# Mixer B's scores: the pass over k's low half as two products of 64 rows, one for each half of the keys

## The chip, the cores and the metric

The kernel runs on one core of one Trainium2 chip. What is measured is the device time of one execution in microseconds; before the change it is 1545.34 us, the median of three runs (1544.65 to 1547.67). On such a core, TensorE (PE) multiplies matrices and transposes, VectorE (DVE), ScalarE (ACT) and GpSimd (POOL) work on tiles, and SyncE (SP) issues DMAs. Each engine runs its own queue of instructions in order and waits for others by semaphores. TensorE reads from SBUF and writes to PSUM, whose banks hold 512 float32 numbers for each of 128 partitions.

## The reference

A trunk of two layers over 1024 tokens of width 1024. Each layer: RMS norm, one projection to q, k, v and a gate, a token mixer, an output projection and a residual, then a gated per-layer embedding. Layer 0 has mixer A (neighbourhood attention), layer 1 has mixer B, which the change touches: 16 query heads of 64 dimensions share 4 heads of k and v, with normalised and rotated q and k.

```python
def q_block(qb):
    sc = jnp.einsum('bkgqd,bksd->bkgqs', qb, k).astype(jnp.float32) * scale
    pr = jax.nn.softmax(sc, axis=-1).astype(v.dtype)
    return jnp.einsum('bkgqs,bksd->bkgqd', pr, v)
```

So for each query head and each block of 128 queries there are 128 x 1024 scores, a softmax over the 1024 keys, and a product with v.

## The kernel before

**Numbers in two parts.** All is float32, but TensorE multiplies in float32r, a rounded float32. Each operand is therefore held as a high part (rounded) and a low part (what the rounding left), and a product is the sum of high by high, high by low and low by high. For most products that is three matmuls (`split3`).

**Mixer B's scores.** A head has only 64 dimensions, and the array has 128 rows, so high and low share them. For each pair of query heads and each half of the queries (`hf`, 512 of them), `q_stack` transposes q, copies it out of PSUM to `raw`, and for each head `j` of the pair fills a tile QS: in the head's own 64 partitions (`own`) ACT writes the high part (line 1068), and two ticks later DVE writes the low part into the other 64 (`oth`, line 1069). On k's side, for each of the 4 KV heads, KA holds k's high part twice, in both halves of the partitions, and KB k's low part twice (`k_stack`; the second copies are POOL's, lines 1005 and 1006). A product of QS with KA over 128 rows then gives (q high + q low) by k high, and one with KB gives (q high + q low) by k low. `f_S` does this for a block of 128 queries: two products of 512 keys each over KA, then two over KB, into a PSUM tile `s` of two banks, one for each 512 keys. All four use the same columns of QS as the stationary operand, and every matmul brings its own weight load.

**The steps.** Mixer B's attention is 128 steps (16 heads, 2 halves of the queries, 4 blocks). At step n PE gets the transposes of P of step n (`f_T`, line 1105), the scores of step n+2 (`f_S`) and at every second step the product with v of the two steps before (`f_AV`, tile `o`). Between them DVE takes the minimum of the scores (they are negated, line 1089), ACT the exponential (line 1095), and both copy the transposed P as high and low part (1107, 1108). `mix` puts dense projections between the attention's items so that both lists end together: the q of the next group, the gates, and the embedding's product. `q_stack` is called 5 steps ahead of the scores that first need it (`QS_AT`); its two high parts are written 4 and 6 ticks later (`QO`), a tick being one item of the attention's list. In the prologue (`pro[0]`) they are written at once.

**POOL's queue in Mixer B** has the rotary products of the next group's q and k (lines 923 to 926), their reciprocal roots and scalings (325, 957), the copies of KA and KB, and for each finished pair of heads the gate and the normalisation of Y (513, 514); the latter waits for a broadcast `rb` that comes through DRAM.

All matmuls except the transposes go through the helper `mm`, so they all have line 317; they are told apart by their tiles: `s` the scores, `d` the projections, `o` mostly the products with v, `t` the transposes.

Of the kernel before, what the change touches and what calls it, by code (L numbers as in the profile page):

```python
# [12 lines left out]
F32R = mybir.dt.float32r  # L13
# [28 lines left out]
QD = (2, 5, 8)  # L42
# [113 lines left out]
def trunk(ctx, tc, x, xT, wts, bias, gains, gain0, hgains, mask, rope, out):  # L156
    nc = tc.nc
    sync, act, dve, pool, pe = nc.sync, nc.scalar, nc.vector, nc.gpsimd, nc.tensor
# [101 lines left out]
    q = WQ.q  # L260
# [55 lines left out]
    def mm(ps, a, b, first, last):  # L316
        pe.matmul(ps, a, b, start=first, stop=last, skip_group_check=True)  # L317
# [560 lines left out]
    def mixer_b(pend):  # L878
        with ExitStack() as es:
# [4 lines left out]
            sb = es.enter_context(tc.tile_pool(name="bsb", bufs=2))  # L884
# [16 lines left out]
            KA, KB, V, QT, QST, P, RS, OP = {}, {}, {}, {}, {}, {}, {}, {}  # L901
# [152 lines left out]
            def q_stack(pair, hf):  # L1054
                g = pair // 2
                ps = psT.tile([128, 4, 128], F32, name="t")
                c = slice((pair % 2) * 128, (pair % 2) * 128 + 128)
                for t in range(4):
                    pe.transpose(ps[:, t], QT[g, hf][:, t, c], ident)  # L1059
                raw = sb.tile([128, 512], F32, name="th")  # L1060
                act.activation(raw, ps.rearrange("p t c -> p (t c)"), AF.Copy)
                for j in range(2):
                    own, oth = slice(64 * j, 64 * j + 64), slice(64 - 64 * j, 128 - 64 * j)
                    qs = sb.tile([128, 512], F32R, name="QS", bufs=3)
                    QST[2 * pair + j, hf] = qs

                    def high(qs=qs, own=own, oth=oth):
                        act.activation(qs[own], raw[own], AF.Copy)
                        post.add(DQ, lambda: dve.tensor_tensor(qs[oth], raw[own], qs[own], ALU.subtract))
                    if pro[0]:  # L1070
                        high()
                    else:
                        post.add(QO[j], high)
# [5 lines left out]
            def f_S(h, hf, t):  # L1079
                g = h // 4  # L1080
                ps = psS.tile([128, 1024], F32, name="s")
                qt = QST[h, hf][:, t * 128:(t + 1) * 128]
                for kk, kt in enumerate((KA[g], KB[g])):
                    for c in range(2):
                        mm(ps[:, c * 512:(c + 1) * 512], qt, kt[:, c * 512:(c + 1) * 512], kk == 0, kk == 1)
                if t == 0:
                    RS[h, hf] = sb.tile([128, 4], F32, name="rs", bufs=3)
                mn = sb.tile([128, 1], F32, name="mn", bufs=3)
                dve.tensor_reduce(mn, ps, axis=AX.X, op=ALU.min)  # L1089
                P[h, hf, t] = (ps, mn)  # L1090
# [38 lines left out]
            pre = kv[:-2] + qi[:6] + kv[-2:-1] + qi[6:10] + kv[-1:] + qi[10:14]  # L1129
            fill = qi[14:] + [d for hf in range(2) for d in gate_items("bg", 0, hf, dalloc, sb, gg)]  # L1130
            pre += [glue(lambda: q_stack(0, 0))] + fill[:5]
            pre += [glue(lambda: f_S(*steps[0]))] + fill[5:6] + [glue(lambda: f_E(*steps[0]))] + fill[6:7]
            pre += [glue(lambda: f_S(*steps[1]))] + fill[7:]
            for i, d in enumerate(pre):
                if i >= 2 and i % 2 == 0 and pend:
# [6 lines left out]
            for g in range(4):  # L1142
                att = []
                for n in range(32 * g, 32 * g + 32):
                    h, hf, t = steps[n]
                    av = n >= 2 and n % 2 == 0
                    w = CB if av else CN
                    att.append((later.tick, w[0]))
                    if av:
                        att.append((lambda n=n: f_AV(*steps[n - 1]), w[1]))  # L1150
                    te = [(lambda n=n: f_T(*steps[n]), w[2])]
                    if n + 1 < len(steps):
                        te.append((lambda n=n: f_E(*steps[n + 1]), w[3]))
                    if n % 2 == 0:
                        te.reverse()
                    att += te
                    if n + 2 < len(steps):
                        att.append((lambda n=n: f_S(*steps[n + 2]), w[4]))
                    m = n + QS_AT
                    if m % 8 == 0 and m < len(steps):  # L1160
                        hn, fn, _ = steps[m]
                        att.append((lambda hn=hn, fn=fn: q_stack(hn // 2, fn), 0.0))
                    if YLOAD_B <= n < YLOAD_B + NT:
                        att.append((lambda t=n - YLOAD_B: load_y(1, t), 0.0))
# [184 lines left out]
```

## Time and profile before

| | before |
|---|---|
| median of 3 runs | 1545.34 us |
| the profiled execution | 1544.88 us |
| its span, from first to last instruction | 1543.1 us |
| mean granted TensorE clock | 0.997 |
| instructions in the trace | 24012 |

The profile is of one execution. Its page gives each engine's busy time, the chain of work that ended last, and groups of instructions by line and tile; the trace behind it can be asked for a stretch of time, for one tile, for waits, or for instructions in order of time. A matmul's duration in the trace runs from its start to a modelled end and overlaps with the next one's; weight loads (PEld) are shown beside the matmuls. The lines that matter are shown in the prediction.

### The profile page before, as it was taken

To read this page: it belongs to the slowest core of one execution; us is meant where nothing else is said; L and a number is where in the kernel's file an instruction comes from. 1 tells how busy PE (TensorE), PEld (TensorE's weight loads), DVE (VectorE), ACT (ScalarE), POOL (GpSimd) and SP (SyncE) were. 2 spreads that over 40 slices of the span, in tenths; PEclk is the share of its full clock that TensorE was granted. 3 is DMA by queue.
4 is the path that set the end of the run, shared out by engine and by line. 5 is a ranking of instruction groups with operands and counts; after the bars stand their busy time and mean duration, and the time that the engine had idled before them with its cause. 6 is when DMAs were issued, how large, how long until landed. Compare 5 with 4: busy or idle time off the path is not lost.

```text
span 1543.1 us, 24012 instructions
## 1 busy us (share of the span) xinstructions
PE 1513.8 (98%) x9016; PEld 1324.3 (86%) x9016; DVE 963.5 (62%) x1638; ACT 847.5 (55%) x1696; POOL 350.6 (23%) x468
## 2 busy tenths in 40 slices
PE   8999999999999999999999999999999999999998
PEld 8789888988988788888988889989899888788886
DVE  4675676566576435556867776677777877624533
ACT  7564555455466423333467676767767767622422
POOL 1231232223122010000432233545041300000124
PEclk9999999999999999999999999999999999999999
DMA  7211312221124961232210111102111213651213
GB/s 300 79 61 47 96 50 67 68 73 60 62 78 124 352 220 44 89 130 79 85 36 22 39 60 41 51 25 69 40 31 42 76 46 118 225 200 55 71 59 130
DMA packets 85635, 138.97 MB, mean 90 GB/s; under 512 B 12816, under 2 KB 49808, under 8 KB 85520
## 3 DMA queue, kind: packets, MB, share of 16 engines
q1 hardware_dynamic: 80912, 122.77, 24.0%
q10 hardware_dynamic: 4608, 14.68, 2.7%
q8 instruction: 71, 1.16, 0.3%
q14 instruction: 44, 0.36, 0.1%
HBM read 104.80 MB, written 32.62 MB: 89 GB/s over the span
## 4 chain that ended last, share of the span: by engine, by line
PE 84%; DVE 6%; ACT 5%; issue 3%; DMA 1%; POOL 1%; ACTq 0%; POOLq 0%; SPq 0%; DVEq 0%
PE d L317 54%; PE o L317 10%; PE s L317 9%; PE t L1105 6%; PE t L686 2%; DVE PTl L1108 1%; PE t L427 1%; DVE mn L1089 1%; ACT PTh L1107 1%; DVE wl L221 1%; ACT P L1095 1%; ACT wh L220 1%; POOL xn L416 1%; PE t L1059 0%; DMA ppD<-G 0%
## 5 line engine op out<-in xcount | busy, mean ns | idle before, releaser
L317 PE MATMUL d<-wh,HTh 128*128 128x256 f32 (+1 forms) x1064 | 358.7, 341 | 5.3 <-ACT wh L232 2.7
L317 PE MATMUL d<-wh,HTl 128*128 128x256 f32 (+1 forms) x1064 | 352.2, 335 | 0.0
L317 PE MATMUL d<-wl,HTh 128*128 128x256 f32 (+1 forms) x1064 | 352.1, 335 | 0.0
L1108 DVE TENSOR_TENSOR PTl<-t,PTh 128x512 fp32r<-128x512 f32 x256 | 164.4, 683 | 124.1 <-ACT PTh L1107 123.6
L317 PEld LDWEIGHTS d<-wh,HTh 128*128 128x128 f32 x1064 | 200.0, 190 | 28.5 <-ACT wh L232 3.0
L317 PEld LDWEIGHTS d<-wl,HTh 128*128 128x128 f32 x1064 | 200.0, 190 | 21.4
L317 PEld LDWEIGHTS d<-wh,HTl 128*128 128x128 f32 x1064 | 199.8, 190 | 21.6
L317 PE MATMUL d<-HTh,wh 128*128 128x512 f32 x504 | 205.7, 408 | 0.0
L317 PE MATMUL d<-HTh,wl 128*128 128x512 f32 x504 | 198.7, 394 | 0.0
L317 PE MATMUL d<-HTl,wh 128*128 128x512 f32 x504 | 197.7, 392 | 0.0
L1095 ACT ACTIVATE P<-s,mn 128x1024 f32<-128x1024 f32 x128 | 142.8, 1115 | 58.2 <-DVE mn L1089 57.5
L1107 ACT ACTIVATE PTh<-t 128x512 fp32r<-128x512 f32 x256 | 139.9, 594 | 43.5 <-PE t L1105 42.5
L1089 DVE TENSOR_REDUCE mn<-s 128x1 f32<-128x1024 f32 x128 | 154.8, 1209 | 11.7 <-PE s L317 11.6
L1105 PE MATMUL t<-ident,P 128*128 128x128 f32 x1024 | 137.4, 275 | 6.7 <-DVE PTl L1108 4.9
L1105 PEld LDWEIGHTS t<-ident,P 128*128 128x128 f32 x1024 | 114.7, 141 | 22.5 <-DVE PTl L1108 16.6
L317 PE MATMUL s<-KA,QS 128*128 128x512 f32 (+2 forms) x384 | 133.7, 402 | 0.0
L221 DVE TENSOR_TENSOR wl<-wstage,wh 128x1024 fp32r<-128x1024 f32 x86 | 107.5, 1255 | 26.7 <-ACT wh L220 25.7
L317 PE MATMUL s<-KB,QS 128*128 128x512 f32 (+2 forms) x384 | 121.6, 371 | 0.0
L317 PE MATMUL o<-PTh,V 128*128 128x256 f32 (+2 forms) x672 | 118.8, 288 | 2.4 <-ACT P L1095 1.1
L317 PE MATMUL o<-PTl,V 128*128 128x256 f32 (+2 forms) x672 | 118.7, 288 | 0.3 <-DVE PTl L690 0.3
L317 PEld LDWEIGHTS d<-HTh,wl 128*128 128x128 f32 x504 | 94.6, 188 | 21.5
L690 DVE TENSOR_TENSOR PTl<-t,PTh 128x384 fp32r<-128x384 f32 (+1 forms) x128 | 66.7, 521 | 65.2 <-ACT PTh L689 63.8
(172 smaller groups left out, 2486.9 us busy)
## 6 DMA issues: line engine op xcount, KB each, us to landing
wstage<-in_wts SPq DMA_DIRECT2D x92, 512.0 KB
X<-in_x SPq DMA_DIRECT2D x16, 512.0 KB
pp<-ppD SPq DMA_DIRECT2D x32, 256.0 KB
rb<-rD SPq DMA_DIRECT2D x56, 128.0 KB
ppD<-th SPq DMA_DIRECT2D x24, 256.0 KB
XT<-in_xT SPq DMA_DIRECT2D x8, 512.0 KB
xD<-X SPq DMA_DIRECT2D x8, 512.0 KB
X<-xD SPq DMA_DIRECT2D x8, 512.0 KB
```

Source lines behind the costliest of these rows:

```text
L220: act.activation(hi, s, AF.Copy)
L221: self.rest = lambda: dve.tensor_tensor(lo, s, hi, ALU.subtract)
L317: pe.matmul(ps, a, b, start=first, stop=last, skip_group_check=True)
L416: pool.tensor_scalar(xns[i][:, :512], xts[i][:, :512], r[:, i:i + 1], None, op0=ALU.mult)
L427: pe.transpose(ps[:, k], xn[:, (4 * c + k) * 128:(4 * c + k + 1) * 128], ident)
L686: pe.transpose(ps[:, i], sp[:, i * 128:(i + 1) * 128], ident)
L690: dve.tensor_tensor(PTl[:, sl], ps[:, :m], PTh[:, sl], ALU.subtract)
L1089: dve.tensor_reduce(mn, ps, axis=AX.X, op=ALU.min)
L1095: act.activation(p, ps, AF.Exp, bias=mn, scale=-1.0, accum_out=RS[h, hf][:, t:t + 1])
L1105: pe.transpose(ps[:, i], p[:, k * 128:(k + 1) * 128], ident)
L1107: act.activation(PTh[:, ks, c], ps, AF.Copy)
L1108: dve.tensor_tensor(PTl[:, ks, c], ps, PTh[:, ks, c], ALU.subtract)
```

## The change

`q_stack` gets one more tile, QD, for a pair of heads: POOL copies each head's high part of q into the other half of the partitions (`qd[oth]` from `qs[own]`), so that a head has its high part in both halves, once in QS and once in QD. In `f_S`, the two products over KA stay. The two over KB become products of 64 rows: the first 512 keys with QS's high part in the head's own half, the other 512 with QD's copy in the other half. They take the high part of q alone, so the product of the two low parts is no longer computed. The last line of the diff makes the reserve in SBUF for DMAs that POOL issues smaller, which makes room for QD's two buffers.

```diff
@@ q_stack
                 act.activation(raw, ps.rearrange("p t c -> p (t c)"), AF.Copy)
+                qd = sb.tile([128, 512], F32R, name="QD", bufs=2)
                 for j in range(2):
                     own, oth = slice(64 * j, 64 * j + 64), slice(64 - 64 * j, 128 - 64 * j)
                     qs = sb.tile([128, 512], F32R, name="QS", bufs=3)
-                    QST[2 * pair + j, hf] = qs
+                    QST[2 * pair + j, hf] = (qs, qd, own, oth)
 
                     def high(qs=qs, own=own, oth=oth):
                         act.activation(qs[own], raw[own], AF.Copy)
+                        pool.tensor_copy(qd[oth], qs[own])
                         post.add(DQ, lambda: dve.tensor_tensor(qs[oth], raw[own], qs[own], ALU.subtract))
@@ f_S
-                qt = QST[h, hf][:, t * 128:(t + 1) * 128]
-                for kk, kt in enumerate((KA[g], KB[g])):
-                    for c in range(2):
-                        mm(ps[:, c * 512:(c + 1) * 512], qt, kt[:, c * 512:(c + 1) * 512], kk == 0, kk == 1)
+                qs, qd, own, oth = QST[h, hf]
+                tc = slice(t * 128, (t + 1) * 128)
+                for c in range(2):
+                    mm(ps[:, c * 512:(c + 1) * 512], qs[:, tc], KA[g][:, c * 512:(c + 1) * 512], True, False)
+                for c, (q, rows) in enumerate(((qs, own), (qd, oth))):
+                    mm(ps[:, c * 512:(c + 1) * 512], q[rows, tc], KB[g][rows, c * 512:(c + 1) * 512], False, True)
@@ kernel
-    nc = bacc.Bacc("TRN2", target_bir_lowering=False, num_devices=1)
+    nc = bacc.Bacc("TRN2", target_bir_lowering=False, num_devices=1, dynamic_dma_scratch_size=1024)
```

On PE the order stays and one row of a step changes. Here is a step in the first group, before: the end of a projection (d), transposes of P, the scores, transposes, and the next projection. Each row is line, operation, output, operands and the output's size.

```order
L317 MATMUL d<-wh_7425,HTl 128x256
L1105 MATMUL t<-ident,P 128x128 x8
L317 MATMUL s<-KA,QS 128x512 x2
L317 MATMUL s<-KB,QS 128x512 x2
L1105 MATMUL t<-ident,P 128x128 x8
L317 MATMUL d<-wh_7768,HTh 128x256
```

The same place after, where the lines behind 1062 have moved by up to four:

```order
L317 MATMUL s<-KA,QS 128x512 x2
L317 MATMUL s<-KB,QS 128x512
L317 MATMUL s<-KB,QD 128x512
L1109 MATMUL t<-ident,P 128x128 x8
L317 MATMUL d<-wh_7771,HTh 128x256
L317 MATMUL d<-wl_7772,HTh 128x256
```

The second product over KB reads QD in place of QS; its output is of the same size, and both now have 64 rows of operands in place of 128.

On POOL, a copy of QD stands behind each of ACT's high parts. Before, at the end of the first group's own attention, POOL has:

```order
L325 TENSOR_TENSOR ss<-ss,neghalf 128x16
L957 TENSOR_TENSOR qt<-qt,ss 128x256 x4
L513 TENSOR_TENSOR Y<-Y,G 128x512
L514 TENSOR_TENSOR Y<-Y,rb 128x512
L513 TENSOR_TENSOR Y<-Y,G 128x512
L514 TENSOR_TENSOR Y<-Y,rb 128x512
L923 TENSOR_TENSOR t_8936<-qt,tab 128x8x16 x2
```

After, at the same place, two copies follow each Y:

```order
L325 TENSOR_TENSOR ss<-ss,neghalf 128x16
L957 TENSOR_TENSOR qt<-qt,ss 128x256 x4
L513 TENSOR_TENSOR Y<-Y,G 128x512
L514 TENSOR_TENSOR Y<-Y,rb 128x512
L1070 COPY QD<-QS 64x512 x2
L513 TENSOR_TENSOR Y<-Y,G 128x512
L514 TENSOR_TENSOR Y<-Y,rb 128x512
L1070 COPY QD<-QS 64x512 x2
L923 TENSOR_TENSOR t_8948<-qt,tab 128x8x16 x2
```

So the copies stand behind line 514, which waits for rb, and ahead of the next rotary products. In the prologue, two copies come ahead of the last copy of KB:

```order
L1005 COPY KA<-KA 64x512
L1006 COPY KB<-KB 64x512
L1005 COPY KA<-KA 64x512
L1070 COPY QD<-QS 64x512 x2
L1006 COPY KB<-KB 64x512
L325 TENSOR_TENSOR ss<-ss,neghalf 128x16
L957 TENSOR_TENSOR qt<-qt,ss 128x256 x4
```

Before, those rows are the same without the copies of QD.

## The prediction

> **What bounds the kernel now.** I read the page's busy times and its chain first, then the stretches of Mixer B, then the rows of the two operands that change. In the page's first part the columns are busy time, share of the span and instructions; in its chain, each engine's and each line's share of the path that ended last.
>
> ```profile
> PE 1513.8 (98%) x9016; PEld 1324.3 (86%) x9016; DVE 963.5 (62%) x1638; ACT 847.5 (55%) x1696; POOL 350.6 (23%) x468
> PE 84%; DVE 6%; ACT 5%; issue 3%; DMA 1%; POOL 1%; ACTq 0%; POOLq 0%; SPq 0%; DVEq 0%
> PE d L317 54%; PE o L317 10%; PE s L317 9%; PE t L1105 6%; PE t L686 2%; DVE PTl L1108 1%; PE t L427 1%; DVE mn L1089 1%; ACT PTh L1107 1%; DVE wl L221 1%; ACT P L1095 1%; ACT wh L220 1%; POOL xn L416 1%; PE t L1059 0%; DMA ppD<-G 0%
> ```
>
> TensorE is the bound, and the score products (tile s, line 317) are 9% of the chain. A share is an average, so the stage is checked next: Mixer B's attention runs from about 774 to 1340 us. Each row gives start:end, length, then busy time of PE, weight loads, DVE, ACT and POOL, granted clock, DMA share and GB/s.
>
> ```profile
> 774.00:930.00 156.00, 152.22 (x1023) 133.68 (x1022) 112.05 (x158) 107.42 (x197) 43.36 (x55) 1.00 0.12 36
> 930.00:1090.00 160.00, 158.81 (x1150) 148.03 (x1149) 112.21 (x163) 113.10 (x222) 71.28 (x116) 1.00 0.16 47
> 1090.00:1240.00 150.00, 147.94 (x1022) 134.63 (x1020) 113.96 (x162) 108.22 (x199) 40.68 (x50) 1.00 0.16 50
> 1240.00:1340.00 100.00, 97.39 (x608) 84.73 (x607) 72.93 (x100) 73.58 (x131) 5.19 (x4) 1.00 0.40 132
> sum 566.00, PE 556.37 PEld 501.07 DVE 411.15 ACT 402.31 POOL 160.52; mean PE 139.09 PEld 125.27 DVE 102.79 ACT 100.58 POOL 40.13
> ```
>
> In every stretch PE is busy 97% or more, DVE and ACT some 72%, POOL 28%, at a granted clock of 1.00. So a microsecond that TensorE saves or loses here moves the end by nearly a microsecond. What PE waits for in 774 to 1340 us (total, times, longest) says how much it is held already:
>
> ```profile
> PE t L1105 <- DVE PTl L1108: 3.8, 4, 1.6
> PE t L1059 <- DVE PTl L1108: 1.3, 3, 0.9
> PE t L1105 <- ACT th L994: 1.1, 2, 0.8
> PE o L317 <- ACT P L1095: 1.1, 1, 1.1
> PE o L462 <- DVE Y L443: 1.0, 1, 1.0
> PE o L317 <- DVE Y L443: 0.2, 1, 0.2
> ```
>
> Those are 8.5 us in all, and none of them is a wait of the score products.
>
> **The change on TensorE.** The groups of 774 to 1340 us with each shape apart count the products (count, busy us, mean ns of one, idle before):
>
> ```profile
> L317 PE MATMUL s<-KA,QS 128*128 128x512 f32 x252 | 86.1, 423 | 0.0
> L317 PE MATMUL s<-KB,QS 128*128 128x512 f32 x253 | 79.4, 394 | 0.0
> ```
>
> Mixer B has 128 steps with two 512-column products over KA and two over KB, so 256 of each (the first step lies ahead of 774 us), and only those over KB change. A duration of 394 ns is not what one costs: matmuls overlap. The cost is the distance between starts, read in the timeline (start, duration, engine, line, operation):
>
> ```profile
> 1004.55 0.28 PE L317 MATMUL d<-wh,HTl 128*128 128x256 f32 x1
> 1004.55 0.31 PEld L317 LDWEIGHTS s<-KA,QS 128*128 128x128 f32 x2
> 1004.67 0.62 PE L317 MATMUL s<-KA,QS 128*128 128x512 f32 x2
> 1004.90 0.42 PEld L317 LDWEIGHTS s<-KB,QS 128*128 128x128 f32 x2
> 1005.13 0.62 PE L317 MATMUL s<-KB,QS 128*128 128x512 f32 x2
> 1005.36 0.19 PEld L317 LDWEIGHTS d<-wh,HTh 128*128 128x128 f32 x1
> 1005.59 0.28 PE L317 MATMUL d<-wh,HTh 128*128 128x256 f32 x1
> 1005.60 0.19 PEld L317 LDWEIGHTS d<-wl,HTh 128*128 128x128 f32 x1
> 1005.71 0.28 PE L317 MATMUL d<-wl,HTh 128*128 128x256 f32 x1
> ```
>
> From the first KB product to what follows it, 1005.13 to 1005.59, are 0.46 us for two, so 0.23 us each; over 128 steps the pass with KB is 58.9 us of PE. The rows show a second thing. A weight load begins when the matmul ahead of it begins (the load for the first KB product at 1004.90, where the second KA product starts; that for d at 1005.36, where the second KB product starts), and the matmul that uses it starts no sooner than 0.11 to 0.12 us later (1004.55 to 1004.67, 1005.60 to 1005.71). The load runs one product ahead and no further. Where products are short it sets the pace:
>
> ```profile
> 1006.91 0.90 PEld L1105 LDWEIGHTS t<-ident,P 128*128 128x128 f32 x8
> 1007.02 1.03 PE L1105 MATMUL t<-ident,P 128*128 128x128 f32 x8
> 1007.78 0.30 PEld L317 LDWEIGHTS s<-KA,QS 128*128 128x128 f32 x2
> 1007.81 0.71 PE L317 MATMUL s<-KA,QS 128*128 128x512 f32 x2
> 1008.36 0.62 PE L317 MATMUL s<-KB,QS 128*128 128x512 f32 x2
> ```
>
> Eight transposes take 0.79 us, 0.099 each; and the two KA products behind them take 0.55 us, 0.09 more than two KB products, since the load at 1007.78 had nothing to hide under.
>
> After the change the KB pass is still two products of 512 columns, each over 64 rows in its own half of the array and into its own PSUM bank. No run here shows such a pair, so its cost is bounded. Above: they run one after the other, 0.46 us, saving nothing. Below: they run at the same time, 0.23 us. Between them lies what the loads allow: the second half's load starts when the first half's product starts, as in every row above, so its product starts 0.12 us later (0.099 by the transposes) and streams 0.23 us: 0.35 us for the pair. I take this middle value because the rule "one load ahead" holds in all the rows. It saves 0.46 - 0.35 = 0.11 us per step, 128 x 0.11 = **14.1 us**.
>
> The other unknown is the handover between whole-array and half-array products, twice per step: into the pair and out of it. The nearest rows are the change from transposes to products above, whose extra 0.09 us is already explained by a load, leaving about zero for the handover itself; and, as an upper end, a full emptying of the array: a product's record lasts 0.39 us and the next starts 0.23 us after it, so waiting for its end would cost 0.16 us. I take zero for the forecast, as nothing in the rows shows a handover between unlike products costing beyond the load, and keep 0.16 us for a rival. The Trainium skill, page "TensorEngine Tiling (Array Packing)", section "Key Properties", says that changing the tiling mode, and not just the tile, drains the engine; no run here shows it, and by that rule the rival below and not the forecast would come out.
>
> **The change elsewhere.** POOL gets 32 copies of 64x512, one behind each of ACT's copies of q's high half. The nearest rows are POOL's copies of KA, the same shape and type; next to them, the tightest of the places where a new q block is first used, its copy on ACT and the products that read it:
>
> ```profile
> L1005 POOL CAST KA<-KA x8: 607/611/967, 751.2 to 1026.9; 64x512 fp32r<-64x512 f32 x8
> 1158.98 0.62 ACT L1068 ACTIVATE QS<-th 64x512 fp32r<-64x512 f32 x1
> 1167.80 0.71 PE L317 MATMUL s<-KA,QS 128*128 128x512 f32 x2
> 857.79 1.29 POOL L514 TENSOR_TENSOR Y<-Y,rb 128x512 f32<-128x512 f32 x1 [5.89 <-DMA rb<-rD]
> 863.95 0.62 ACT L1068 ACTIVATE QS<-th 64x512 fp32r<-64x512 f32 x1
> 1075.81 2.33 POOL L957 TENSOR_TENSOR qt<-qt,ss 128x256 f32<-128x256 f32 x4
> 1088.03 0.60 PE L1059 MATMUL t<-ident,qt 128*128 128x128 f32 x4
> 765.19 0.81 POOL L1006 CAST KB<-KB 64x512 fp32r<-64x512 f32 x1
> 763.20 1.29 ACT L1068 ACTIVATE QS<-th 64x512 fp32r<-64x512 f32 x2
> ```
>
> 32 x 0.61 = 19.6 us go to a POOL that is busy 160.5 of 566 us. ACT is done at 1159.60, so the copy would end at about 1160.2, and PE reads the block at 1167.80 at the earliest: 7.6 us of cover. In the queue the copy stands behind Y's product with rb (L514), which waits up to 6 us for a DMA; but that ended at 859.08, while ACT made its block only at 863.95, so the copy is not held by it. If it ever were, PE would wait for the part over 7.6 us. Queued behind the copies is the work on the next group's q. Its last scaling (L957) ends 9.9 us before the transposes that read it, at the nearest place I found (1078.14 to 1088.03), and two copies put it back by 1.2 us. In the prologue two copies come ahead of the last copy of KB (765.19) and delay it by some 1.3 us; that one belongs to the second KV group, first read 32 steps later. ACT and DVE issue the same instructions as before. The DMA scratch that is made smaller belongs to transfers that POOL issues, and the page's DMA list has only SP's and ACT's, so it costs and gains nothing. All this I take at **0**, with 0 and about 1 us as ends.
>
> **The sum.** The profiled execution took 1544.88 us (1543.1 of span and 1.8 around it), 0.5 us below the median of 1545.34. From 14.1 us saved, I give back 2 us: with PE sooner at the transposes, some of the waits of 8.5 us grow, since they hang on ACT and DVE, whose work is unchanged; ends are 0 and 8.5 us (all of them doubled). 1544.9 - 14.1 + 2.0 = 1532.8; with the median's 0.5 us **1533**. Its own range, with loads of 0.099 to 0.12 us, 0 to 8.5 us given back: 1528 to 1540.
>
> **Rivals.**
> *Both halves at once.* If the second half's load need not wait for the first half's product, the pair costs 0.23 us: 128 x 0.23 = 29.4 us less, 2 given back, 1518. Against it: no load in the rows runs two ahead; for it: the two halves' weights don't share rows. The skill's page "TensorE: Matmul & The Clock Gate", section "The mechanism", has products in unlike row groups start about 4 ns apart, which would make this one; no run here shows it.
> *The array empties at each change.* Place: ahead of the first half product, and ahead of whatever follows the second. At 0.16 us each, 0.32 per step stand against 0.11 saved: 128 x 0.21 = 27 us more, 1572. If the weight load is held as well, 0.12 more each time, it is 128 x 0.45 = 58 us, 1603. It decides from 0.055 us per change on, where loss and gain are equal. For it: no row has such a change, so nothing but a product's record bounds it. Against it: the one change of kind that the trace has, from transposes to products, costs no more than its load.
> *One after the other.* The change says two halves of the array, but if the products queue for it, or if the handover takes just the 0.055 us, the time stays within 1542 to 1548.
> *A late copy on POOL* would show as waits of PE for line 1070; the cover above leaves it 0.02, inside the others.
>
> **How the numbers follow.** Forecast 0.34; both at once 0.13; even 0.15; emptying at up to 0.16 us 0.22, with the loads held 0.16. About 0.2% (3 us) is what a measurement of this kernel can tell from no change. Faster: 0.34 + 0.13 = 0.47; same 0.15; slower 0.38. The range takes in both halves at once (1518, with nothing given back 1516, rounded down to 1515) and the emptying without the loads (1572, with 1 us for POOL and rounding 1575), and leaves out the last case, 0.16. The forecast's own range is 1528 to 1540.
>
> **What would show it.** In the changed timeline, the start of s<-KB,QD against that of s<-KB,QS (0.12 us later: forecast; at once: first rival; 0.23 or more: queueing); the start of the first half product against the second KA product (0.23: no handover; 0.39: emptied), and of what follows the pair against its second product (0.23 or 0.39 again). Weight loads of the halves should start with the matmul ahead. POOL's line 1070 should show 32 copies of about 0.61 us, with no wait of PE on it. The prediction is wrong if either handover is over 0.055 us, whatever the pair itself does.

## The result and the profile after

The change makes the kernel slower: 1560.61 us (median of 4 runs, 1559.77 to 1564.57) against 1546.51 us before, measured beside it; the ratio is 1.0095, with a 95% interval of 1.007 to 1.0119. That is 14.1 us more where 12 less were forecast. The profiled execution took 1559.77 us, its span 1558.0.

The page's busy times after:

```profile
PE 1529.7 (98%) x9016; PEld 1292.9 (83%) x9016; DVE 966.3 (62%) x1638; ACT 847.4 (54%) x1696; POOL 370.9 (24%) x500
```

PE's busy time grew by 15.9 us, the span by 14.9; ACT's busy time did not change, DVE's grew by 2.8 us, and POOL has its 32 copies. From the first product with KA in Mixer B to the last one, by their starts in the trace, it was 567.7 us before and is 581.6 us: 14.0 us, so nearly all of the loss lies in this stage. The stage starts 0.8 us later, and behind it both kernels take 198.6 to 198.8 us to the end of PE's work.

Here is the place in the timeline of after that answers to the one in the prediction (the scores between two projections; start, duration, engine, line, operation, and in brackets what ended idle time):

```profile
1010.64 0.28 PE L317 MATMUL d<-wh,HTl 128*128 128x256 f32 x1
1010.64 0.31 PEld L317 LDWEIGHTS s<-KA,QS 128*128 128x128 f32 x2
1010.76 0.63 PE L317 MATMUL s<-KA,QS 128*128 128x512 f32 x2
1011.32 0.18 PEld L317 LDWEIGHTS s<-KB,QS 64*128 64x128 f32 x1 [0.37 <-issue]
1011.32 0.49 PE L317 MATMUL s<-KB,QS 64*128 64x512 f32 x1
1011.32 0.18 PEld L317 LDWEIGHTS s<-KB,QD 64*128 64x128 f32 x1
1011.32 0.50 PE L317 MATMUL s<-KB,QD 64*128 64x512 f32 x1
1011.75 0.19 PEld L317 LDWEIGHTS d<-wh,HTh 128*128 128x128 f32 x1 [0.25 <-issue]
1011.75 0.38 PE L317 MATMUL d<-wh,HTh 128*128 128x256 f32 x1
1011.86 0.19 PEld L317 LDWEIGHTS d<-wl,HTh 128*128 128x128 f32 x1
1011.97 0.28 PE L317 MATMUL d<-wl,HTh 128*128 128x256 f32 x1
```

Three things are to be seen. First, the two half products start together, and so do their loads: the pair does take the time of one. Second, neither load starts together with the second KA product, as the loads did before. That product started at 1010.99 (0.23 behind the first), so it would have handed over at 1011.22; the loads start at 1011.32, **0.10 us later, in which nothing starts**. Third, a matmul that is issued together with its own load has a longer record: 0.49 where a product of 512 columns had 0.39, and 0.38 where one of 256 columns had 0.28. I read this **0.10 us as the load, now exposed**; the run with the pair twice, below, bears this out. Behind the pair the same happens again: the load for d stands at 1011.75, not under the pair, and the second d product comes 0.22 us behind the first in place of 0.12. From the first KA product to the second d product it was 1.04 us before (1004.67 to 1005.71) and is 1.21 us now.

Over all 128 steps, the median distances between starts (ns) in the two traces, by what PE does ahead of the scores and behind them (KA1 and KA2 are the two products over KA, KB1 the first one over KB, next, second and third the matmuls behind the scores, d the projections):

```
ahead, behind              steps  KA1-KA2  KA2-KB1  KB1-next  next-second  KA1-third behind
before transposes, d          68      315      232       465          227              1465
after  transposes, d          68      315      327       428          333              1629
before d, transposes          19      231      232       462          108              1154
after  d, transposes          19      240      322       434          165              1265
before transposes twice       13      315      232       741          164              1560
after  transposes twice       13      315      327       638          165              1557
```

The entry costs 95 ns more, the pair saves only 37 ns to the next start, and the next product is 106 ns late (57 where transposes follow): 0.16 us a step. Where PE waits behind the scores in any case (the last two rows), the surcharge is hidden in the wait. 68 x 0.164 + 19 x 0.111, and 23 steps of other kinds at 0.15 to 0.17, make 16.9 us. Added up step by step instead of by medians, these distances grew by 15.8 us, while everything between them became 1.7 us shorter; PE's idle time in the stage fell by 0.9 us (9.6 to 8.7). So the stage lost 14.0.

The products over KB in the groups of 774 to 1355 us (count, busy us, mean ns of one, idle before), and PE's waits there (total, times, longest):

```profile
L317 PE MATMUL s<-KB,QS 64*128 64x512 f32 x127 | 62.7, 494 | 0.0
L317 PE MATMUL s<-KB,QD 64*128 64x512 f32 x127 | 62.6, 493 | 0.0
...
PE t L1109 <- DVE PTl L1112: 3.0, 3, 1.4
PE t L1059 <- DVE PTl L1112: 1.5, 3, 0.9
PE o L317 <- ACT P L1099: 1.2, 1, 1.2
PE o L462 <- DVE Y L443: 0.9, 1, 0.9
PE t L1109 <- ACT th L994: 0.9, 2, 0.5
```

The waits came to 7.5 us, from 8.5, and none is for POOL.

### The profile page after: what moved, and what is told of

Same layout as the page of the kernel before. It is cut to its first block, busy times and chain, and to the rows that moved or that the text cites. A ratio compares the mean times of both kernels' runs of the same rounds, so it can differ in the third digit from the quotient of the medians.

```text
span 1558.0 us, 24058 instructions
## 1 busy us (share of the span) xinstructions
PE 1529.7 (98%) x9016; PEld 1292.9 (83%) x9016; DVE 966.3 (62%) x1638; ACT 847.4 (54%) x1696; POOL 370.9 (24%) x500
## 4 chain that ended last, share of the span: by engine, by line
PE 84%; DVE 6%; ACT 5%; issue 2%; DMA 1%; POOL 1%; ACTq 0%; POOLq 0%; SPq 0%; DVEq 0%
PE d L317 55%; PE o L317 10%; PE s L317 9%; PE t L1109 6%; PE t L686 2%; DVE PTl L1112 2%; PE t L427 1%; ACT PTh L1111 1%; DVE mn L1093 1%; DVE wl L221 1%; ACT P L1099 1%; POOL xn L416 1%; ACT wh L220 1%; PE t L1059 0%; DMA ppD<-G 0%
## 5 line engine op out<-in xcount | busy, mean ns | idle before, releaser
L317 PE MATMUL d<-wh,HTh 128*128 128x256 f32 (+1 forms) x1064 | 362.4, 344 | 4.9 <-ACT wh L232 2.3
L317 PE MATMUL d<-HTh,wh 128*128 128x512 f32 x504 | 209.0, 415 | 0.0
L317 PE MATMUL d<-HTh,wl 128*128 128x512 f32 x504 | 198.6, 394 | 0.0
L317 PEld LDWEIGHTS d<-HTh,wh 128*128 128x128 f32 x504 | 94.8, 188 | 19.6 <-issue 7.2
```

## The experiments

**Theory 1 (changeover, or handover as the prediction calls it):** each change between whole-array and half-array products costs PE about 0.2 us, 0.1 in which nothing starts (the hold) and 0.1 for a load that is no longer hidden. **Theory 2:** half-array products are dear in themselves. **Theory 3:** POOL's copies, or the places of the tiles, cost the time. Four kernels tell them apart.

**The copies alone.** Against the changed kernel:

```diff
-                for c, (q, rows) in enumerate(((qs, own), (qd, oth))):
-                    mm(ps[:, c * 512:(c + 1) * 512], q[rows, tc], KB[g][rows, c * 512:(c + 1) * 512], False, True)
+                for c in range(2):
+                    mm(ps[:, c * 512:(c + 1) * 512], qs[:, tc], KB[g][:, c * 512:(c + 1) * 512], False, True)
```

> The changed kernel with the two products over KB put back to 128 rows; the 32 copies of QD on POOL and the smaller scratch stay (QD is read by nobody). Theory 1 (changeover: each change between whole-array and half-array products costs TensorE about 0.2 us, 0.1 us in which nothing may start and 0.1 us for a weight load that is no longer hidden): no half-array product is left, so the time is that of the kernel before, 1546 +- 3 us. Theory 2 (half-array products are dear in themselves, whatever stands beside them): the same, 1546. Theory 3 (the copies on POOL, PE's wait for them, or the moved tiles cost the time): 1560 us as in the changed kernel.

Measured: 1547.31 us, ratio to before 1.0002 (0.9993 to 1.0012). Theory 3 falls: the copies and the smaller scratch cost nothing that can be measured. (PE does not wait for QD here; in the changed kernel it never showed a wait for it.)

**Both half products on the same half.**

```diff
-                for c, (q, rows) in enumerate(((qs, own), (qd, oth))):
+                for c, (q, rows) in enumerate(((qs, own), (qs, own))):
```

> The changed kernel, but the second key half's product reads the head's own half too (QS and KB in the same 64 partitions), so that the two cannot run at once; QD is read by nobody. Theory 1: still two changeovers per step, and the pair streams 0.46 us in place of 0.23: 128 x 0.23 = 29 us over the changed kernel, 1590 us, 43 us over the kernel before; in the trace the second half product starts 0.23 us after the first as it is seen, and the hold of 0.1 us before the pair and behind it stays. Theory 2, in the form that two halves running at once hinder each other: about 0.46 us for the pair without the surcharge, 1546 to 1550 us.

Measured: 1583.33 us, ratio 1.0233 (1.0212 to 1.0253). This is the direct price of the changeovers, since the products stream as long as those of before. In its timeline (transposes ahead, first KA product at 1006.40):

```profile
1007.04 0.29 PEld L317 LDWEIGHTS s<-KB,QS 64*128 64x128 f32 x2 [0.37 <-issue]
1007.04 0.73 PE L317 MATMUL s<-KB,QS 64*128 64x512 f32 x2
1007.69 0.19 PEld L317 LDWEIGHTS d<-wh,HTh 128*128 128x128 f32 x1 [0.36 <-ACT PTh L1111]
1007.70 0.39 PE L317 MATMUL d<-wh,HTh 128*128 128x256 f32 x1
...
1007.92 0.28 PE L317 MATMUL d<-wl,HTh 128*128 128x256 f32 x1
```

The second half product's load is hidden under the first one (two loads within 0.29 us); only at the two changes are the hold and the late load seen. In the 68 steps between transposes and d, the five distances from the first KA product to the second product behind the scores sum to 1636 ns, against 1239 before: **0.40 us for two changeovers**. The stage took 605.1 us, 37.4 more than before, so 0.29 us a step on the average, since some steps hide it. Theory 1 expected 1590 and left out that 18 steps wait behind the scores in any case and hide the surcharge; in the 13 of them with transposes on both sides the distance from the first KA product to the third start behind the scores grew by only 19 ns (1560 to 1579). That two halves running at once hinder each other, which would have brought this run back to 1546 to 1550 us, is ruled out: running them one after the other is 22.7 us slower than together.

**The pair twice**, one behind the other:

```diff
+                for c, (q, rows) in enumerate(((qs, own), (qd, oth))):
+                    mm(ps[:, c * 512:(c + 1) * 512], q[rows, tc], KB[g][rows, c * 512:(c + 1) * 512], False, False)
                 for c, (q, rows) in enumerate(((qs, own), (qd, oth))):
                     mm(ps[:, c * 512:(c + 1) * 512], q[rows, tc], KB[g][rows, c * 512:(c + 1) * 512], False, True)
```

> The changed kernel with the pair of half products run twice in each step, one pair behind the other (the low part of k is added twice). Theory 1: no changeover between the pairs, so the second pair costs its stream alone, 0.23 us x 128 = 29 us: 1590 us. Theory 2: each pair costs the 0.64 us or so that the first one does (0.43 from its start to the next load, and the 0.2 of late start): 128 x 0.6 = 77 us more, about 1637 us.

Measured: 1584.1 us, ratio 1.0237 (1.0217 to 1.0258), 23.5 us over the changed kernel, where theory 1 expected 29: the stream of a second pair and no surcharge. In the 68 steps between transposes and d the distance from the first KA product to the second product behind the scores grew by 0.236 us (1400 to 1636 ns), and in the 13 steps that wait between transposes by 0.024. Theory 2 (1637) falls. The timeline shows the second pair's loads 0.11 us behind the first's, under it, and its records back at 0.39:

```profile
1007.18 0.50 PE L317 MATMUL s<-KB,QS 64*128 64x512 f32 x1
...
1007.19 0.50 PE L317 MATMUL s<-KB,QD 64*128 64x512 f32 x1
1007.29 0.19 PEld L317 LDWEIGHTS s<-KB,QS 64*128 64x128 f32 x1
1007.29 0.19 PEld L317 LDWEIGHTS s<-KB,QD 64*128 64x128 f32 x1
1007.52 0.39 PE L317 MATMUL s<-KB,QS 64*128 64x512 f32 x1
1007.53 0.39 PE L317 MATMUL s<-KB,QD 64*128 64x512 f32 x1
1007.84 0.19 PEld L317 LDWEIGHTS d<-wh,HTh 128*128 128x128 f32 x1 [0.36 <-ACT PTh L1113]
```

**The pair first.**

```diff
-                for c in range(2):
-                    mm(ps[:, c * 512:(c + 1) * 512], qs[:, tc], KA[g][:, c * 512:(c + 1) * 512], True, False)
                 for c, (q, rows) in enumerate(((qs, own), (qd, oth))):
-                    mm(ps[:, c * 512:(c + 1) * 512], q[rows, tc], KB[g][rows, c * 512:(c + 1) * 512], False, True)
+                    mm(ps[:, c * 512:(c + 1) * 512], q[rows, tc], KB[g][rows, c * 512:(c + 1) * 512], True, False)
+                for c in range(2):
+                    mm(ps[:, c * 512:(c + 1) * 512], qs[:, tc], KA[g][:, c * 512:(c + 1) * 512], False, True)
```

> The changed kernel with the pair ahead of the two products over KA (start and stop flags moved with them). Two changeovers per step as before. Theory 1: behind transposes (86 of 128 steps) the first product's load is late by 0.09 us in any case, so there the change into the pair adds only the hold: 86 x 0.09 = 8 us less than the changed kernel, 1552 us; the change out of the pair is now always into KA and costs 0.2 us, also in the 19 steps in which transposes follow at once, 1 us back: 1553 us. Theory 2: the order does not matter, 1560 us.

Measured: 1562.53 us, ratio 1.0098 (1.0083 to 1.0113): no gain, where I expected 1553. The number is the one that theory 2 gave, but the trace shows why theory 1 was reckoned wrongly here. By the starts in its trace, a half product comes 203 ns behind the start of a transpose, 209 ns behind a product of 256 columns and 322 ns behind one of 512; transposes follow each other at 109, products of 256 at 120, of 512 at 230 (medians). So the hold is about 0.09 us behind each kind, and the late load comes on top of it behind transposes too; but leaving for KA now costs the full price in all 128 steps, where before 32 left for transposes.

**Fewer changeovers.** If the changes cost and the pairs don't, two steps' pairs in a row should win. The scores of two steps are issued together, first in the kernel before, as a control, then with the pairs, then with the scores right ahead of a step's transposes:

```diff
-                    if n + 2 < len(steps):
-                        att.append((lambda n=n: f_S(*steps[n + 2]), w[4]))
+                    if n % 2 == 0 and n + 2 < len(steps):
+                        att.append((lambda n=n: f_SS(steps[n + 2], steps[n + 3]), CB[4] + CN[4]))
...
+            def f_SS(*both):
+                made = [f_KA(*s) for s in both]
+                for s, ps in zip(both, made):
+                    f_KB(*s, ps)
+                for s, ps in zip(both, made):
+                    f_min(*s, ps)
```

where `f_KA`, `f_KB` and `f_min` are the three parts of the changed `f_S`; the control calls the old `f_S` twice. The third kernel issues the two steps' scores in front of `f_T` at odd steps, in one item with it.

> The control of the next run: the kernel before (whole-array products), with the scores of two steps issued together at every second step instead of one step's at every step. All theories: the same products, so 1546.8 us, give or take 5 for the waits that the other order makes or saves.

> The changed kernel with the scores of two steps issued together: four products over KA, then the two pairs of half products behind each other, so 64 times two changeovers in place of 128 times two; the products are those of the changed kernel. Theory 1 (the changeover costs): the changed kernel's 14.1 us over 128 steps are what two changeovers cost less 0.23 us, so two changeovers cost 0.34 us on the average; here 64 x (0.34 - 2 x 0.23) = 8 us less than the control, about 1539 us if the control is at 1546.8. Rival (the surcharge goes with each pair, not with the change): 14 us over the control, about 1561 us.

> As the run with two steps' pairs together, and the scores now stand right ahead of a step's transposes, so that the change out of half-array products is always into transposes. Theory 1: in the changed kernel the product behind the first one after the pair comes 0.11 us later than before where projections or V products follow, 0.06 us where transposes follow; 64 x 0.05 = 3 us less than the run before this one, about 1536 us; unless DVE and ACT, which now get the scores of two steps at another place, make PE wait more. Rival: no difference to the run before.

Measured: the control 1577.75 us (ratio 1.019, 1.0169 to 1.0211), the pairs 1581.31 us (1.0216, 1.0196 to 1.0236), ahead of the transposes 1568.86 us (1.0141, 1.0116 to 1.0166). The grouping itself costs 30 us against an expectation of 5 at most. Most of it is waits: PE's idle time between the first and the last score product is 9.6 us in the kernel before, 32.1 in the control and 39.6 with the pairs. On PE alone theory 1 holds: the median distance from the first KA product to the second start behind the scores fell in all three kinds of place where two steps' scores stand, from 1973 ns in the control to 1850 with the pairs where projections stand ahead and transposes behind (11 places), from 2170 to 2104 where it is the other way round (40), and from 1982 to 1915 between projections (12). The rival wanted more than the control. That is some 5 us in all; the 8 us expected rested on 0.34 us for two changeovers, in place of 0.40. But the time did not follow. PE's largest waits in 770 to 1375 us, of the control:

```profile
PE o L317 <- DVE Y L443: 11.4, 10, 2.6
PE t L1059 <- DVE PTl L1108: 9.0, 7, 1.9
PE o L317 <- ACT PTh L1107: 4.5, 8, 1.0
```

and of the kernel with the pairs:

```profile
PE t L1059 <- DVE PTl L1130: 14.3, 9, 2.5
PE o L317 <- DVE Y L443: 11.8, 10, 2.3
PE o L317 <- ACT PTh L1129: 4.7, 8, 1.0
PE s L317 <- ACT P L1117: 2.3, 5, 0.6
```

In these two profiled executions (1573.21 and 1582.91 us, further apart than the medians) the waits grew by more than PE gained. The 8 us were not seen, the two ratios' intervals overlap, and the expectation missed; so no time measured here shows a gain from fewer changeovers, only PE's own distances do. The third kernel's gain over the second, 12 us, is larger than the 3 us expected, PE's idle time is 31.5 us there, and how much of the gain is the cheaper changeover and how much are other waits stays open. None of them beats the kernel before.

**Is PE's time the kernel's time?** Two kernels leave work out of the kernel before: the whole pass over KB, and a quarter of its columns.

```diff
-                for kk, kt in enumerate((KA[g], KB[g])):
-                    for c in range(2):
-                        mm(ps[:, c * 512:(c + 1) * 512], qt, kt[:, c * 512:(c + 1) * 512], kk == 0, kk == 1)
+                for c in range(2):
+                    mm(ps[:, c * 512:(c + 1) * 512], qt, KA[g][:, c * 512:(c + 1) * 512], True, True)
```

> The kernel before without the pass over k's low part (256 products of 512 columns left out). It tests the premise that TensorE's time here is the kernel's time: 128 x 0.46 = 58.9 us less, 1488 us, and a few us more where waits for DVE and ACT grow, up to 1497. If ACT or DVE were the bound of the stage, the time would stay above 1515 us.

```diff
-                        mm(ps[:, c * 512:(c + 1) * 512], qt, kt[:, c * 512:(c + 1) * 512], kk == 0, kk == 1)
+                        e = c * 512 + (512, 384)[kk]
+                        mm(ps[:, c * 512:e], qt, kt[:, c * 512:e], kk == 0, kk == 1)
```

> The kernel before with the products over KB cut from 512 to 384 columns each (the low part of k is left out for a quarter of the keys). A product of 384 columns takes 0.056 us less by the columns' share, 256 x 0.056 = 14 us of TensorE, which is what the prediction wanted the half-array pair to save. Premise of the prediction (2 us given back): 1536 us. By the run without the low pass, where 59 us of TensorE gave 27 us of time: 14 x 0.45 = 6 us less, 1541 us.

Measured: 1521.29 us without the pass (ratio 0.983, 0.9806 to 0.9853), 26.8 us for 58.9 us of PE. My expectation of 1488 to 1497 us missed, and the sign set beforehand for DVE or ACT as the bound, a time above 1515 us, came out: for so large a saving PE alone is not the bound. With 384 columns it is 1539.69 us (0.9954, 0.9937 to 0.9972), 7.2 us for 14.7 us of PE (the distance of the products over KB falls from 232 to 174.5 ns, 256 times), near the 6 us of the second reckoning. PE's waits, without the pass in 770 to 1375 us:

```profile
PE t L1104 <- DVE PTl L1107: 18.2, 26, 2.4
PE t L1059 <- DVE PTl L1107: 3.3, 5, 0.7
PE o L317 <- DVE Y L443: 2.8, 4, 1.1
```

and with 384 columns in 774 to 1350 us:

```profile
PE t L1106 <- DVE PTl L1109: 8.2, 18, 1.8
PE t L1106 <- ACT th L994: 1.3, 2, 1.0
```

and of the kernel before, in 770 to 1375 us:

```profile
PE t L1105 <- DVE PTl L1108: 4.9, 5, 1.6
```

The transposes of P wait until DVE has emptied the transpose buffers: 4.9 us in 5 waits over the whole stage before, 8.2 in 18 with 384 columns, 18.2 in 26 without the pass. By the distances between starts, most of what the stage did not gain lies ahead of transposes: 5.2 of 7.1 us with 384 columns, 21.9 of 32.6 without the pass. In these two runs a saving on PE in this stage arrived by half or less; of a loss, most arrived (14.0 of 15.8 us in the changed kernel).

## Why the prediction was wrong

**The step that failed** is the one on the handover: "I take zero for the forecast, as nothing in the rows shows a handover between unlike products costing beyond the load, and keep 0.16 us for a rival." Two changeovers cost 0.40 us where nothing hides them (both half products on the same half), against 0.23 us that the pair saves. The inference from transposes to products was of the wrong kind: both use all 128 rows, so those rows hold no change of rows at all. The absence of evidence was read as zero. The rows were also misread in size: the transposes follow each other at 0.109 us and not 0.099, since the record of the first KA product starts 0.028 us behind the last of them and is 0.09 us longer than the others (0.479). That moves the low end of the forecast's own range by about 1 us and nothing else. The Trainium skill, page "TensorEngine Tiling (Array Packing)", section "Key Properties", says that a change of the tiling mode drains the engine. The trace agrees with that rule in that nothing starts for 0.10 us at a change. The other 0.10 us, the exposed load, is a term that the prediction had only for the case in which loads are held.

**The rival "the array empties at each change"** had both places and the sign. Its size was put together otherwise: 0.16 us for waiting until a product's record ends, against 0.11 saved. Measured are 0.20 per change against 0.23 saved, which makes 0.40 - 0.23 = 0.17 us a step, and 14.1 us in all since some steps hide it; the forecast of that case was 27. That 1560.6 us lies between the named ends, 1515 and 1575, is owed to this rival and not to the forecast's own sum (1528 to 1540), and in part to luck: both terms came out larger than reckoned, with opposite signs.

**The pair** was mis-sized the other way: "one load ahead" was taken to set the second product 0.12 us behind the first. The two loads and the two products start together, within 3 ns by the median, so "both halves at once" was right on this term. The Trainium skill, page "TensorE: Matmul & The Clock Gate", section "The mechanism", has about 4 ns between such starts. The trace agrees with that figure, with its 3 ns.

**What was given back** was mis-sized as well: 2 us were taken for 14.1 saved, and the run with 384 columns gave back 7.5 of 14.7. Busy shares of 72% for DVE and ACT were read as room; but the waits behind DVE's copies of P grew in both runs in which PE gained (4.9, 8.2 and 18.2 us). By the share of the run with 384 columns, an estimate, the gain would have been some 7 us and not 12 even with the handover at zero and the pair as forecast.

**Right:** that the sign follows PE's time, that POOL's copies and the moved tiles cost nothing that can be measured (ratio 1.0002), that PE does not wait for QD, and that ACT and DVE keep their work. The signs named in advance did point at the cause: a half product comes 0.33 us behind the second KA product, between the 0.23 of no handover and the 0.39 of an emptied array, so the handover is over 0.055 us; and the loads of the halves do not start with the matmul ahead.

## What to carry to other kernels

By PE's own distances here, half-array products pay only in a row: each time PE changes to half-array products and back, the pairs between the two changes have to earn both of them (0.40 us where nothing hides them; a pair of 512 columns saves 0.23). Two pairs in a row saved PE 0.07 to 0.12 us, but no order of the work tried here turned that into time, since grouping the scores cost more in waits. Ask of each new kind of neighbour whether the trace has that very change; if not, let the range and the likeliest case carry its cost. Before crediting PE with savings in a stage where it is 97% busy, take a little work off PE in a test run and see what arrives: here half of a saving was lost, most of it in waits.

## What the runs showed of the hardware

A change of the rows in use is not priced by the end of the matmul's record: behind products of 512 and 256 columns and behind transposes the first half product came 0.09 to 0.10 us later than the next matmul of the same kind would have, though those records last 0.39, 0.28 and 0.28 us. In this time no load starts, not even one for the rows that are about to be used; within one mode the loads are hidden for half products as for whole ones (0.11 us apart in the run with the pair twice). Without the low pass, the granted clock in 1240 to 1330 us was 0.96 (1.00 before), in a stretch in which PE was busy 82.35 of 90 us. The loss sits in two stretches of 10 us at 0.83 (1290 to 1300 and 1310 to 1320 us, PE busy 8.29 and 8.73 us). With 384 columns PE was busy only 8.21 us in 1320 to 1330 us at a clock of 1.00, so PE's busy share alone does not decide it, and what does stays open. The rows of the kernel before and of the one without the low pass:

```profile
1240.00:1330.00 90.00, 88.95 (x557) 77.68 (x556) 65.97 (x90) 66.15 (x118) 5.19 (x4) 1.00 0.37 123
1240.00:1330.00 90.00, 82.35 (x497) 69.42 (x496) 61.85 (x88) 64.07 (x114) 2.59 (x2) 0.96 0.45 153
```
